# Seven block products for three of eight quads of the gate and up projections, five smaller feed-forward parts, and a scheduler that orders the feed-forward instructions

## The chip, the cores and the metric

The kernel runs on one core of a Trainium2 chip. The metric is the time of one execution on the device in microseconds (us); the median of several runs is given. A profile is one more execution, recorded by the hardware profiler. Engines are called PE (TensorE, matrix products), DVE (VectorE), ACT (ScalarE), POOL (GpSimd) and SP (SyncE, which issues the loads here).

## The reference

One layer of a transformer encoder on 256 tokens of 2048 features, all in float32. The first sub-layer mixes tokens (latent attention and dilated attention, gated and projected). The second, which the change is about, is a feed-forward block with 5632 hidden columns:

```python
gt, up = jnp.split(rms_norm(x, g_ffn) @ w_gate_up, 2, axis=-1)
return x + (jax.nn.silu(gt) * up) @ w_down
```

`w_gate_up` is 2048 x 11264 (the gate's 5632 columns, then the up columns), `w_down` is 5632 x 2048.

## The kernel before, in words

All float32 products are made of three matmuls. Each operand is cut in a high part of type float32r and a low part, which is what the cast left out. `mm3` (L383) multiplies high by high, high by low and low by high into one PSUM bank; the low by low term is left out.

Every weight product is a `Group`: up to 512 columns of a weight matrix, the list of its blocks of 128 rows (k), the transposed activation it multiplies and an `evac` function for the finished sums. A group holds two PSUM banks, one for each half of 128 tokens (the tag `main`, two tiles in turn, so that one group's sums can be read while the next ones grow). Groups are cut into chunks of two k: 512 KB of weights. `load(i)` (L694) issues a chunk's transfer on SP's queue. `split(i)` (L705) casts it on ACT (L710, the high part) and subtracts on DVE (L711, the low part). `products(i)` (L718) issues its 12 matmuls of 128x512 on PE: two k, two token halves, three matmuls. Loads run four chunks ahead of the products and splits three. There are four raw buffers, four for high parts and four for low ones; SP waits with a load until DVE has subtracted from the buffer's old content.

The feed-forward block comes last. The normalised activation is not scaled before the product; the row factor `st["2"]` is applied when the sums are read. `evac_wo` (L568) adds the residual to form `x1`, and a job transposes `x1` into `hT`, four feature blocks at a time (L201, eight transposes into a bank pair with the tag `side`). The 5632 hidden columns are worked through in 11 strips of 512, in two parts of six and five strips (`halves`). Each strip is a gate group of 16 k and an up group of 16 k. `evac_gate` (L592) applies Silu to the gate's sums on ACT, `evac_up` (L600) multiplies by the up sums on DVE, and a job transposes the result (the tile `tr_hid`, eight transposes) and cuts it into high and low parts (L171, L176). After a part's strips come four groups of `w_down`, 512 output columns each, whose k are the hidden blocks of that part; `evac_down` adds their sums to `x1`.

The order of all instructions is written out by hand: `tc.manual_schedule()` keeps every engine's instructions in the order of the program text, and the loop at the end of `layer_kernel` goes through the chunks, advancing at most one pending job after each.

Of the kernel before, what the change touches and what calls it, by code (L numbers as in the profile page):

```python
# [19 lines left out]
P = 128  # L20
# [17 lines left out]
CK = 2  # L38
AHEAD = 3
# [29 lines left out]

class Flag:  # L70
# [11 lines left out]
def layer_kernel(ctx: ExitStack, tc: tile.TileContext, a: dict, out: bass.AP):  # L82
    nc = tc.nc
    cp = ctx.enter_context(tc.tile_pool(name="cp", bufs=1))
    wp = ctx.enter_context(tc.tile_pool(name="wp", bufs=AHEAD + 1))
    tp = ctx.enter_context(tc.tile_pool(name="tp", bufs=34))
# [3 lines left out]
    ctx.enter_context(tc.manual_schedule())  # L90
# [4 lines left out]
    def small(shape, name):  # L95
        return cp.tile(shape, F32, name=name)

# [81 lines left out]

    class Act:  # L180
        """hi and lo parts of a transposed activation, in tiles of 4 blocks."""
# [14 lines left out]
    def transpose_in(act, k0, nk, src, gname=None):  # L196
        """blocks k0..k0+nk (nk <= 4, in one tile of act) from src(t, k) [tok, 128]."""
# [142 lines left out]
    def rope(x, A, B, nh, i):  # L340
        """x [P, NT, nh, 64] rotated in place, with the gain in the tables."""
# [46 lines left out]
    def job_attn(kind, p):  # L388
# [29 lines left out]
        # transposes of q and k  # L418
# [21 lines left out]
        # scores  # L440
# [28 lines left out]
        # transposes of the probabilities  # L469
# [8 lines left out]
        # values  # L478
# [8 lines left out]
    def job_prep_dil(n):  # L487
        """the norms of all heads: keys are scaled, the queries' factor waits for the scores"""
# [72 lines left out]
    x1, hT, hjobs, xres = {}, Act("hT", KD), {}, {}  # L561
    ss2 = small([P, NT, 4], "ss2")

    def load_xres(j):
        xres[j] = t4([P, NT, 512], f"xres{j}")
        nc.sync.dma_start(xres[j], xd[:, :, j * 512:(j + 1) * 512])

    def evac_wo(j):  # L568
        def evac(ps, step):
# [6 lines left out]
            def job():  # L576
                transpose_in(hT, 4 * j, 4, lambda t, k: x1[j][:, t, (k % 4) * P:(k % 4 + 1) * P], "g_ffn")
                return
                yield
            hjobs[j] = Job(job())  # L580
            hjobs[j].ready = step + 2
            jobs.append(hjobs[j])
# [7 lines left out]
    sg, hidT, djobs = {}, {}, {}  # L590

    def evac_gate(half, i):  # L592
        def evac(ps, step):
            z = t4([P, NT, 512], f"sg{half}_{i}")
            for t in range(NT):
                nc.scalar.activation(z[:, t], ps[:, t], AF.Silu, scale=st["2"][:, t:t + 1])
            sg[half, i] = z
        return evac

    def evac_up(half, i):  # L600
        def evac(ps, step):
            z = sg[half, i]
            for t in range(NT):
                nc.vector.scalar_tensor_tensor(z[:, t], ps[:, t], st["2"][:, t:t + 1], z[:, t], op0=ALU.mult, op1=ALU.mult)

            def job():
                transpose_in(hidT[half], 4 * i, 4, lambda t, k: z[:, t, (k % 4) * P:(k % 4 + 1) * P])
                return
                yield
            djobs[half, i] = Job(job())  # L610
            djobs[half, i].ready = step + 2
            jobs.append(djobs[half, i])
        return evac

    def evac_down(half, j):
        def evac(ps, step):
            nc.vector.tensor_add(x1[j], ps, x1[j])
            if half == 1:
# [20 lines left out]
    g_in(0, 512, evac_lat("cq"), sizes=[1, 1, 2, 2, 2, 2, 2, 2, 2])  # L639
# [28 lines left out]
    halves = (range(0, 6), range(6, 11))  # L668
    for half, js in enumerate(halves):
        hidT[half] = Act(f"hid{half}", 4 * len(js))  # L670
        for i, j in enumerate(js):
            nh = {k: (lambda k=k: [hjobs[k // 4]]) for k in range(KD)}
            groups.append(Group(W["w_gate_up"], 512 * j, 512, range(KD), hT, evac_gate(half, i), nh))
            groups.append(Group(W["w_gate_up"], DFF + 512 * j, 512, range(KD), hT, evac_up(half, i), nh))
# [5 lines left out]
    chunks = []  # L680
    for gi, g in enumerate(groups):
        ks, sizes = list(g.ks), list(g.sizes or [])
        while ks:
            n = sizes.pop(0) if sizes else CK
            chunks.append((g, gi, ks[:n], ks[0] == g.ks[0], len(ks) <= n))
            ks = ks[n:]

    wt, parts, gps = {}, {}, {}
    first_chunk = {}
    for i, c in enumerate(chunks):  # L690
        first_chunk.setdefault(c[1], i)
    early = {}

    def load(i):  # L694
        g, gi, ks, _, _ = chunks[i]
        if gi == 0 and i:
# [3 lines left out]
        t = wp.tile([P, len(ks), g.n], F32, name=f"w{i}", tag="w")  # L700
        src = g.w[ks[0] * P:(ks[-1] + 1) * P, g.c0:g.c0 + g.n]
        nc.sync.dma_start(t, src.rearrange("(k p) n -> p k n", p=P))
        wt[i] = t

    def split(i):  # L705
        g, gi, ks, _, _ = chunks[i]
        t = wt.pop(i)
        h = wp.tile([P, len(ks), g.n], F32R, name=f"wh{i}", tag="wh")
        l = wp.tile([P, len(ks), g.n], F32R, name=f"wl{i}", tag="wl")
# [146 lines left out]
```

## Time and profile before

| | |
|---|---|
| median of three runs | 1368.96 us (1368.63 to 1369.15) |
| profiled execution, span from the first to the last instruction | 1367.5 us |
| PE busy | 1356.5 us (99%) |
| DVE busy | 758.1 us (55%) |
| ACT busy | 623.5 us (46%) |
| read from HBM | 253.97 MB (187 GB/s over the span, writes included) |
| granted TensorE clock | 1.000 |

The profiled execution's own time is known by its span alone; the span leaves out what lies before the first and after the last instruction. Busy times are sums of an engine's instruction durations. A matmul's end is modelled and matmuls overlap, so PE's pace is read from the distance of their starts.

### The profile page before, as it was taken

How to read it: one execution, taken by the hardware profiler on the slowest of the kernel's cores; microseconds unless marked ns; L12 is line 12 of the kernel's file. 1: busy time of each engine (PE TensorE's matmuls, PEld its weight loads, DVE VectorE, ACT ScalarE, POOL GpSimd, SP SyncE). 2: the span in 40 equal slices, each digit the busy share in tenths (PEclk: the TensorE clock that was granted, in tenths of full speed). 3: DMA queues.
4: the chain of work that ended last, by engine and by line, in shares of the span. 5: the costliest groups of instructions: out<-in, count | busy, mean ns of one | idle time of the engine just before them, and what ended most of it. 6: DMA issues, size and time to landing. Idle time of an engine off the chain costs nothing.

```text
span 1367.5 us, 16361 instructions
## 1 busy us (share of the span) xinstructions
PE 1356.5 (99%) x6342; PEld 1144.7 (84%) x6342; DVE 758.1 (55%) x774; ACT 623.5 (46%) x776; POOL 32.3 (2%) x41
## 2 busy tenths in 40 slices
PE   7999999999999999999999999999999999999998
PEld 6899999888888888888888888888888888888887
DVE  5566777677655556555445544554444544555443
ACT  6555655454444444445444444433344444444332
POOL 1011111000000000000000000000000000000000
PEclk9999999999999999999999999999999999999999
DMA  8555555555566666565665665555665665565663
GB/s 259 175 173 168 158 172 177 174 166 172 178 202 199 198 190 216 193 210 181 196 192 182 191 198 184 187 189 193 194 193 187 194 197 188 186 188 183 202 212 123
DMA packets 138205, 257.14 MB, mean 188 GB/s; under 512 B 9192, under 2 KB 28688, under 8 KB 138128
## 3 DMA queue, kind: packets, MB, share of 16 engines
q1 hardware_dynamic: 137760, 255.96, 59.8%
q8 instruction: 49, 0.80, 0.2%
q14 instruction: 28, 0.23, 0.0%
q10 hardware_dynamic: 144, 0.13, 0.0%
q0 software_dynamic: 224, 0.01, 0.0%
HBM read 253.97 MB, written 2.10 MB: 187 GB/s over the span
## 4 chain that ended last, share of the span: by engine, by line
PE 99%; DMA 1%; SPq 0%; DVE 0%; issue 0%; ACT 0%; DVEq 0%
PE g L384 31%; PE g L386 31%; PE g L385 31%; PE tr_hid L201 1%; DMA w<-in_w_in_dram 1%; PE tr_hT L201 0%; PE tr_mT L201 0%; PE tr_xT L201 0%; DMA xn<-in_x_dram 0%; PE mla3s L386 0%; PE mla2s L386 0%; PE mla0s L386 0%; PE mla1s L386 0%; PE mla2s L385 0%; PE mla2s L384 0%; PE mla1s L385 0%
## 5 line engine op out<-in xcount | busy, mean ns | idle before, releaser
L711 DVE TENSOR_TENSOR wl<-w,wh 128x1024 fp32r<-128x1024 f32 (+2 forms) x481 | 575.6, 1201 | 472.8 <-ACT wh L710 470.8
L710 ACT CAST wh<-w 128x1024 fp32r<-128x1024 f32 (+2 forms) x481 | 496.2, 1036 | 537.6 <-PE g L386 489.7
L384 PE MATMUL g<-wh,hTh 128*128 128x512 f32 x704 | 274.8, 390 | 0.0
L386 PE MATMUL g<-wh,hTl 128*128 128x512 f32 x704 | 274.0, 389 | 0.0
L385 PE MATMUL g<-wl,hTh 128*128 128x512 f32 x704 | 273.9, 389 | 0.0
L384 PE MATMUL g<-wh,xTh 128*128 128x512 f32 (+1 forms) x544 | 210.2, 386 | 1.9 <-ACT xTh L173 1.9
L386 PE MATMUL g<-wh,xTl 128*128 128x512 f32 (+1 forms) x544 | 207.2, 381 | 0.5 <-DVE xTl L178 0.5
L385 PE MATMUL g<-wl,xTh 128*128 128x512 f32 (+1 forms) x544 | 207.2, 381 | 0.0
L386 PEld LDWEIGHTS g<-wh,hTl 128*128 128x128 f32 x704 | 132.1, 188 | 27.6
L385 PEld LDWEIGHTS g<-wl,hTh 128*128 128x128 f32 x704 | 132.2, 188 | 27.1
L384 PEld LDWEIGHTS g<-wh,hTh 128*128 128x128 f32 x704 | 132.2, 188 | 27.1
L384 PEld LDWEIGHTS g<-wh,xTh 128*128 128x128 f32 x544 | 102.7, 189 | 17.2 <-ACT xTh L173 2.1
L386 PEld LDWEIGHTS g<-wh,xTl 128*128 128x128 f32 x544 | 102.4, 188 | 17.3 <-DVE xTl L178 1.0
L385 PEld LDWEIGHTS g<-wl,xTh 128*128 128x128 f32 x544 | 102.6, 189 | 15.3 <-DVE wl L711 0.4
L384 PE MATMUL g<-wh,hid0h 128*128 128x512 f32 x192 | 74.8, 390 | 0.0
L386 PE MATMUL g<-wh,hid0l 128*128 128x512 f32 x192 | 74.7, 389 | 0.0
L385 PE MATMUL g<-wl,hid0h 128*128 128x512 f32 x192 | 74.7, 389 | 0.0
L384 PE MATMUL g<-wh,hid1h 128*128 128x512 f32 x160 | 62.3, 390 | 0.0
L386 PE MATMUL g<-wh,hid1l 128*128 128x512 f32 x160 | 62.2, 389 | 0.0
L385 PE MATMUL g<-wl,hid1h 128*128 128x512 f32 x160 | 62.2, 389 | 0.0
L384 PE MATMUL g<-wh,mTh 128*128 128x512 f32 x128 | 50.2, 392 | 0.0
L386 PE MATMUL g<-wh,mTl 128*128 128x512 f32 x128 | 49.8, 389 | 0.0
(509 smaller groups left out, 1233.5 us busy)
## 6 DMA issues: line engine op xcount, KB each, us to landing
w<-in_w_gate_up_dram SPq DMA_DIRECT2D x176, 512.0 KB, 4.5
w<-in_w_down_dram SPq DMA_DIRECT2D x88, 512.0 KB, 4.3
w<-in_w_in_dram SPq DMA_DIRECT2D x79, 512.0 KB, 4.2
w<-in_w_in_dram SPq DMA_DIRECT2D x56, 448.0 KB, 3.6
w<-in_w_o_dram SPq DMA_DIRECT2D x32, 512.0 KB, 4.5
w<-in_w_o_mla_dram SPq DMA_DIRECT2D x16, 512.0 KB, 4.1
w<-in_w_o_dil_dram SPq DMA_DIRECT2D x16, 512.0 KB, 4.2
w<-in_w_ukv_dram SPq DMA_DIRECT2D x8, 512.0 KB, 4.3
```

The source lines that it names most:

```text
L201: nc.tensor.transpose(ps[:, k, t * P:(t + 1) * P], src(t, k0 + k), ident)
L384: nc.tensor.matmul(ps, ah, bh, start=first, stop=False)
L385: nc.tensor.matmul(ps, ah, bl, start=False, stop=False)
L386: nc.tensor.matmul(ps, al, bh, start=False, stop=last)
L710: nc.scalar.copy(h, t)
L711: nc.vector.tensor_sub(l, t, f32(h))
```

## The change

The feed-forward block is rearranged; the arithmetic of everything before it stays.

- Gate and up of a strip become one group, a *pair*. Its work is cut into eight *quads*: two feature blocks by two token halves on the activation's side, two feature blocks by gate and up on the weights' side. That is a product of two 2 x 2 block matrices. Five quads are done plainly with eight block products. Three (`FAST`, quads 2, 4 and 6) are done with seven block products of sums and differences of blocks (Winograd's form of Strassen's method), each still three matmuls. The last quad, 7, is a plain one.
- The sums and differences of the activation's blocks are made once, in `job_h`. Those of the weights are made for each fast quad in `split_fast`: four adds of 512 elements on DVE, in place in the raw buffer, after the two right-hand blocks and one left-hand block were cut into high and low parts.
- A pair holds all eight PSUM banks (`hold_banks`): four for the ordinary sums, into which three of the seven products go too, and four shared by the other products of the three fast quads. `evac_fast` combines the shared four, placed after the last fast quad; `evac_pair` adds the result to the ordinary four, then applies Silu and multiplies.
- Five parts of 3, 2, 2, 2 and 2 strips take the place of two of 6 and 5. Down groups use the held banks, two groups chunk by chunk in turn (not the very last two).
- A feed-forward chunk is 1 MB (a quad, or four k of `w_down`) in two transfers. There are three raw buffers of 1 MB, and six of the same size for high and low parts. Before the feed-forward block a chunk stays 512 KB; there it uses half of a raw buffer, and one of the six buffers holds its high and low part. The working tiles `t4` go from 34 to 28.
- From the third of the four `w_o` groups on the hand-written order ends (`in_order.close()`): the framework's scheduler orders the instructions of each engine by their place in the text, their readiness and a priority, which is raised by `PRIO` for the combining.

```diff
-CK = 2
-AHEAD = 3
+CK = 4
+AHEAD = 2
+PARTS = ((0, 3), (3, 5), (5, 7), (7, 9), (9, 11))
+PRIO = 200
+NPAIR = KD // 2
+FAST = (2, 4, 6)
...
+class Quad:
+    def __init__(self, group, i):
+        self.group, self.i, self.fast = group, i, i in FAST
+        plain = [k for k in range(NPAIR) if k not in FAST]
+        self.first, self.last = i == plain[0], i == plain[-1]
+        self.first_fast, self.last_fast = i == FAST[0], i == FAST[-1]
...
-    wp = ctx.enter_context(tc.tile_pool(name="wp", bufs=AHEAD + 1))
-    tp = ctx.enter_context(tc.tile_pool(name="tp", bufs=34))
+    tp = ctx.enter_context(tc.tile_pool(name="tp", bufs=28))
+    xp = ctx.enter_context(tc.tile_pool(name="xp", bufs=3))
+    wp = ctx.enter_context(tc.tile_pool(name="wp", bufs=6))
     sp = ctx.enter_context(tc.tile_pool(name="sp", bufs=4))
     psm = ctx.enter_context(tc.tile_pool(name="psm", bufs=2, space=PSUM))
     pss = ctx.enter_context(tc.tile_pool(name="pss", bufs=2, space=PSUM))
-    ctx.enter_context(tc.manual_schedule())
+    in_order = ctx.enter_context(ExitStack())
+    in_order.enter_context(tc.manual_schedule())
...
+    def half_side(name):
+        if not held:
+            return side(name)[:, :512]
+        spare.rotate(-1)
+        return held["q"][spare[-1]]
+    def hold_banks():
+        for n in "AB":
+            held[n] = psm.tile([P, NT, 512], F32, name=f"m{n}", tag="main")
+        for n in "CD":
+            held[n] = side(f"s{n}").rearrange("p (t n) -> p t n", t=NT)
+        held["q"] = {m: held[n][:, i] for n, ms in (("A", (1, 6)), ("B", (7, 5)), ("C", (3, 2)), ("D", (4, 0)))
+                     for i, m in enumerate(ms)}
+        spare.extend((1, 6, 7, 5))
...
+    def split_pair(h, l, x):
+        nc.scalar.copy(h, x)
+        nc.vector.tensor_sub(l, x, f32(h))
...
+    def job_h(i):
+        ps = half_side(f"tr_h{i}").rearrange("p (k s) -> p k s", s=S)
+        for k in range(2):
+            f = 2 * i + k
+            for t in range(NT):
+                nc.tensor.transpose(ps[:, k, t * P:(t + 1) * P], x1[f // 4][:, t, (f % 4) * P:(f % 4 + 1) * P], ident)
+        g = [gain("g_ffn", 2 * i + k) for k in range(2)]
+        if i not in FAST:
+            hP[i] = t4([P, 2, 2, S], f"hP{i}", F32R)
+            split_evac(*((hP[i][:, 0, k], hP[i][:, 1, k], ps[:, k], g[k]) for k in range(2)))
+        else:
+            v, l, h = t4([P, 8, P], f"hs{i}"), t4([P, 7, P], f"hsl{i}", F32R), t4([P, 7, P], f"hsh{i}", F32R)
+            nc.scalar.activation(v[:, 0:8:7], ps[:, 0].rearrange("p (t s) -> p t s", t=NT), AF.Copy, scale=g[0])
+            nc.scalar.activation(v[:, 1:3], ps[:, 1].rearrange("p (t s) -> p t s", t=NT), AF.Copy, scale=g[1])
+            nc.vector.tensor_sub(v[:, 3], v[:, 7], v[:, 2])
+            nc.vector.tensor_sub(v[:, 4], v[:, 7], v[:, 0])
+            nc.vector.tensor_sub(v[:, 5], v[:, 0], v[:, 3])
+            nc.vector.tensor_sub(v[:, 6], v[:, 1], v[:, 5])
+            split_pair(h, l, v[:, :7])
+            hq[i] = (h, l)
...
+    def evac_fast(q):
+        bank, z, u = held["q"], t4([P, NT, 512], f"z{q.group.c0}"), t4([P, NT, 512], f"u{q.group.c0}")
+        add, sub = nc.vector.tensor_add, nc.vector.tensor_sub
+        with tc.high_priority(offset=PRIO):
+            nc.scalar.copy(u[:, 0], bank[1])
+            sub(z[:, 0], bank[6], u[:, 0])
+            add(u[:, 1], bank[7], z[:, 0])
+            add(z[:, 1], bank[5], u[:, 1])
+            add(z[:, 0], bank[5], z[:, 0])
+        q.group.zu = z, u
+    def evac_pair(half, i, last):
+        def evac(zu, step):
+            q = held["q"]
+            z, u = zu
+            add, sub = nc.vector.tensor_add, nc.vector.tensor_sub
+            with tc.high_priority(offset=PRIO):
+                add(z[:, 1], q[0], z[:, 1])
+                add(z[:, 0], q[3], z[:, 0])
+                add(u[:, 0], q[2], u[:, 0])
+                sub(u[:, 1], q[4], u[:, 1])
+            r = st["2"]
+            for t in range(NT):
+                nc.scalar.activation(z[:, t], z[:, t], AF.Silu, scale=r[:, t:t + 1])
+            for t in range(NT):
+                nc.vector.scalar_tensor_tensor(z[:, t], u[:, t], r[:, t:t + 1], z[:, t], op0=ALU.mult, op1=ALU.mult)
 
             def job():
-                transpose_in(hidT[half], 4 * i, 4, lambda t, k: z[:, t, (k % 4) * P:(k % 4 + 1) * P])
+                ps = held["D" if last else "A"].rearrange("p t (k s) -> p (t k) s", s=S)
+                for k in range(4):
+                    for t in range(NT):
+                        nc.tensor.transpose(ps[:, k, t * P:(t + 1) * P], z[:, t, k * P:(k + 1) * P], ident)
+                h, l = hidT[half].tiles(i)
...
+            needs = {k: (lambda k=k: [hjobs[k]]) for k in range(NPAIR)}
+            needs[FAST[0]] = lambda: list(hjobs.values())
+            if i:
+                needs[FAST[0]] = lambda half=half, i=i: [djobs[half, i - 1]]
+            groups.append(Group(W["w_gate_up"], 512 * j, 1024, range(NPAIR), None, evac_pair(half, i, i == len(js) - 1), needs))
...
+        elif gi >= ffn_at:
+            for two in (gi, gi + 2):
+                for a_, b_ in zip(chunk_ks(groups[two], two), chunk_ks(groups[two + 1], two)):
+                    if two + 2 == len(groups):
+                        continue
+                    add_chunk(two, a_)
+                    add_chunk(two + 1, b_)
+            if two + 2 == len(groups):
+                for e in (two, two + 1):
+                    for ks in chunk_ks(groups[e], e):
+                        add_chunk(e, ks)
+            gi += 3
...
+    def load(c):
+        g, gi, ks, q = chunks[c]
+        t = xt[c] = xp.tile([P, 4, 512], F32, name=f"x{c}", tag="x")
+        if q:
+            for kk in range(2):
+                src = g.w[(2 * q.i + kk) * P:(2 * q.i + kk + 1) * P].rearrange("p (n f) -> p n f", n=2)
+                nc.sync.dma_start(t[:, 2 * kk:2 * kk + 2], src[:, :, g.c0:g.c0 + 512])
+            return
...
+    def split_fast(c):
+        x = xt[c]
+        rh, rl, r = (t4([P, 2, 512], f"{n}{c}", F32R) for n in ("rh", "rl", "r"))
+        split_pair(rh, rl, x[:, 2:4])
+        split_pair(r[:, 0], r[:, 1], x[:, 1])
+        add = nc.vector.tensor_add
+        add(x[:, 1], x[:, 0], x[:, 1])
+        add(x[:, 0], x[:, 0], x[:, 2])
+        add(x[:, 2], x[:, 1], x[:, 2])
+        add(x[:, 3], x[:, 2], x[:, 3])
+        raws[c] = {1: (r[:, 0], r[:, 1]), 3: (rh[:, 0], rl[:, 0]), 2: (rh[:, 1], rl[:, 1])}
+    def split(c):
+        g, gi, ks, q = chunks[c]
+        if q and q.fast and c not in raws:
+            split_fast(c)
+        t = xt.pop(c)
+        h = w8(f"wh{c}")
+        h, l = (h, w8(f"wl{c}")) if gi >= ffn_at else (h[:, :2], h[:, 2:])
+        s = (slice(None), slice(0, 4 if q else len(ks)), slice(0, 512 if q else g.n))
+        split_pair(h[s], l[s], t[s])
+        if q and q.fast:
+            parts[c] = raws.pop(c) | {m: (h[:, n], l[:, n]) for n, m in enumerate((7, 5, 6, 4))}
+        else:
+            parts[c] = (h, l)
...
+    FACTOR = {1: 0, 2: 1, 4: 2, 5: 3, 7: 4, 6: 5, 3: 6}
+    PLAIN = {(0, 0): 3, (0, 1): 2, (1, 0): 0, (1, 1): 4}
+    def products_quad(c):
+        q = chunks[c][3]
+        bank, w = held["q"], parts.pop(c)
+        if not q.fast:
+            h, l = w
+            for t, n in ((1, 0), (0, 0), (0, 1), (1, 1)):
+                m = PLAIN[t, n]
+                for kk in range(2):
+                    s = slice(t * P, (t + 1) * P)
+                    mm3(bank[m], hP[q.i][:, 0, kk, s], hP[q.i][:, 1, kk, s], h[:, 2 * kk + n], l[:, 2 * kk + n],
+                        q.first and kk == 0, q.last and kk == 1)
+        else:
+            h, l = hq[q.i]
+            for m in (1, 6, 7, 5, 3, 2, 4):
+                f = FACTOR[m]
+                mm3(bank[m], h[:, f], l[:, f], *w[m], q.first_fast and m in (1, 5, 6, 7), q.last_fast and m in (1, 5, 6, 7))
+        if q.last_fast:
+            evac_fast(q)
+        return getattr(q.group, "zu", None)
+    DOWN = "ABCA"
...
+            ps = held[DOWN[g.c0 // 512]]
...
+    def splits(to):
+        while ahead["split"] < min(to, n):
+            c = ahead["split"]
+            loads(c + 1)
+            if c + 1 < n and chunks[c + 1][3] and chunks[c + 1][3].fast and c + 1 not in raws:
+                loads(c + 2)
+                split_fast(c + 1)
+            split(c)
+            ahead["split"] += 1
...
+        if first and gi == ffn_at - 2:
+            in_order.close()
         for fn in early.get(i, ()):
             fn()
-        if i + AHEAD + 1 < n:
-            load(i + AHEAD + 1)
-        if i + 1 < n and chunks[i][1] == 0:
+        if ks[0] == allks[0]:
+            loads(c + AHEAD + 2)
+        if i + 1 < len(steps) and gi == 0:
             for j in needs_of(i + 1):
                 j.finish(i)
         for j in needs_of(i):
             j.finish(i)
-        if i + AHEAD < n:
-            split(i + AHEAD)
+        if ks[0] == allks[0]:
+            ahead_of = c + AHEAD + 1 + (gi < ffn_at - 1)
+            splits(ahead_of)
+            loads(ahead_of + 2)
+        if gi == ffn_at and not held:
+            hold_banks()
```

## Rows read from the trace of the kernel before

**Rows 1.** The page's busy times: us, share of the span, instructions.
```profile
PE 1356.5 (99%) x6342; PEld 1144.7 (84%) x6342; DVE 758.1 (55%) x774; ACT 623.5 (46%) x776; POOL 32.3 (2%) x41
```
**Rows 2.** The page's chain that ended last, share of the span by engine.
```profile
PE 99%; DMA 1%; SPq 0%; DVE 0%; issue 0%; ACT 0%; DVEq 0%
```
**Rows 3.** Stretches: us, busy (instructions) PE, PEld, DVE, ACT, POOL; clock; DMA; GB/s.
```profile
60.00:1363.00 1303.00, 1303.00 (x6105) 1102.37 (x6104) 724.32 (x725) 588.82 (x714) 26.07 (x23) 1.00 0.60 187
...
907.00:950.00 43.00, 43.00 (x193) 35.65 (x192) 21.26 (x18) 17.79 (x17) 0.00 (x0) 1.00 0.59 189
```
**Rows 4.** The chain in order of time, two sets of transposes: start, us, what.
```profile
862.14 0.87 PE tr_hid L201 x8
...
906.55 0.87 PE tr_hid L201 x8
```
**Rows 5.** The page's groups, feed-forward matmuls: out<-in, count, busy us, mean ns.
```profile
L384 PE MATMUL g<-wh,hTh 128*128 128x512 f32 x704 | 274.8, 390 | 0.0
L386 PE MATMUL g<-wh,hTl 128*128 128x512 f32 x704 | 274.0, 389 | 0.0
L385 PE MATMUL g<-wl,hTh 128*128 128x512 f32 x704 | 273.9, 389 | 0.0
...
L384 PE MATMUL g<-wh,hid0h 128*128 128x512 f32 x192 | 74.8, 390 | 0.0
...
L384 PE MATMUL g<-wh,hid1h 128*128 128x512 f32 x160 | 62.3, 390 | 0.0
```
**Rows 6.** Waits: who waited for whom, us in total, times, longest us.
```profile
ACT wh L710 <- PE g L386: 489.7, 322, 4.4
DVE wl L711 <- ACT wh L710: 470.8, 330, 7.0
```
**Rows 7.** Groups by form, DVE: count, busy us, mean ns, idle before.
```profile
L711 DVE TENSOR_TENSOR wl<-w,wh 128x1024 fp32r<-128x1024 f32 x415 | 506.6, 1224 | 457.0 <-ACT wh L710 455.7
...
L604 DVE SCALAR_TENSOR_TENSOR sg<-g,r,sg 128x512 f32<-128x512 f32 x22 | 15.5, 747 | 4.6 <-PE g L386 4.6
...
L617 DVE TENSOR_TENSOR x<-g,x 128x1024 f32<-128x1024 f32 x7 | 8.6, 1224 | 2.9 <-PE g L386 2.9
...
L711 DVE TENSOR_TENSOR wl<-w,wh 128x512 fp32r<-128x512 f32 x2 | 1.4, 692 | 1.3 <-ACT wh L710 1.3
```
**Rows 8.** Groups by form, ACT: the same columns.
```profile
L710 ACT CAST wh<-w 128x1024 fp32r<-128x1024 f32 x415 | 436.1, 1054 | 511.7 <-PE g L386 465.3 <-DMA w<-in_w_down_dram 28.9 <-DMA w<-in_w_in_dram 10.9
...
L596 ACT ACTIVATE sg<-g,r 128x512 f32<-128x512 f32 x22 | 13.9, 686 | 16.7 <-PE g L386 16.7
...
L173 ACT ACTIVATE hTh<-tr_hT,gcol 128x256 fp32r<-128x256 f32 x16 | 6.3, 475 | 7.3 <-PE tr_hT L201 7.3
L171 ACT CAST hid0h<-tr_hid 128x1024 fp32r<-128x1024 f32 x6 | 6.1, 1018 | 15.3 <-PE tr_hid L201 15.3
...
L710 ACT CAST wh<-w 128x512 fp32r<-128x512 f32 x2 | 1.2, 616 | 1.2 <-DMA w<-in_w_in_dram 1.2
```
**Rows 9.** Timeline, DVE around 901 and 1362 us: start, us, instruction.
```profile
901.15 1.41 DVE L604 SCALAR_TENSOR_TENSOR sg<-g,r,sg 128x512 f32<-128x512 f32 x2 [0.41 <-PE g L386]
...
1362.14 0.69 DVE L626 TENSOR_TENSOR x<-g,x 128x512 f32<-128x512 f32 x1 [6.47 <-PE g L386]
```
**Rows 10.** Waits of SP's queue, the longest: us in total, times, longest us.
```profile
SPq L702 <- DVE wl L711: 1008.2, 442, 5.6
```
**Rows 11.** Transfers: KB each, median us to landing; then GB/s in 0:40 us.
```profile
w<-in_w_gate_up_dram SPq DMA_DIRECT2D x176, 512.0 KB, 4.5
...
GB/s 0 8 157 298 185 142 262 313 323 388 394 388 383 375 376 368 379 370 374 375 378 385 227 168 346 98 281 156 53 238 344 67 50 144 258 195 287 195 272 197
```
**Rows 12.** Timeline of SP's queue, the fourth and fifth weight load: start, us.
```profile
4.63 0.47 SPq L702 DMA_DIRECT2D w<-in_w_in_dram  x1
...
6.11 0.86 SPq L702 DMA_DIRECT2D w<-in_w_in_dram  x1
```

More of the change, by code (lines that the diff above doesn't have):

```diff
@@ L678, in layer_kernel, with add_chunk @@
                                 {k: (lambda k=k, half=half: [djobs[half, k // 4]]) for k in range(4 * len(js))}))
-    chunks = []
-    for gi, g in enumerate(groups):
-        ks, sizes = list(g.ks), list(g.sizes or [])
+    chunks, steps = [], []
+    def add_chunk(gi, ks, q=None):
+        g = groups[gi]
+        c = len(chunks)
+        chunks.append((g, gi, ks, q))
+        if q:
+            steps.append((c, ks, ks[0] == g.ks[0], ks[-1] == g.ks[-1]))
+            return
+        for o in range(0, len(ks), 2):
+            sub = ks[o:o + 2]
+            steps.append((c, sub, sub[0] == g.ks[0], sub[-1] == g.ks[-1]))
@@ L694, in load @@
-    def load(i):
-        g, gi, ks, _, _ = chunks[i]
-        if gi == 0 and i:
+        return r
+    gi = 0
+    while gi < len(groups):
+        g = groups[gi]
+        if g.n == 1024:
+            for i in g.ks:
+                add_chunk(gi, [i], Quad(g, i))
+        elif gi >= ffn_at:
[11 more added lines that the diff above has]
+        else:
+            for ks in chunk_ks(g, gi):
+                add_chunk(gi, ks)
+        gi += 1
@@ L699, in load @@
                 load_rows()
[L700 to L709, printed above, removed]
-        nc.scalar.copy(h, t)
-        nc.vector.tensor_sub(l, t, f32(h))
-        parts[i] = (h, l)
+        for o in range(0, len(ks), 2):
+            sub = ks[o:o + 2]
+            src = g.w[sub[0] * P:(sub[-1] + 1) * P, g.c0:g.c0 + g.n]
+            nc.sync.dma_start(t[:, o:o + len(sub), :g.n], src.rearrange("(k p) n -> p k n", p=P))
@@ L718, in products @@
+    DOWN = "ABCA"
     def products(i):
-        g, gi, ks, first, last = chunks[i]
+        c, ks, first, last = steps[i]
+        g, gi, allks, q = chunks[c]
+        if q:
+            return products_quad(c)
         final = gi == len(groups) - 1
-        if first and not final:
+        if first and gi < ffn_at:
             ps = psm.tile([P, NT, 512], F32, name=f"g{gi}", tag="main")
@@ L770, in layer_kernel, with loads @@
     n = len(chunks)
-    for i in range(min(AHEAD + 1, n)):
-        load(i)
+    ahead = {"load": 0, "split": 0}
+    def loads(to):
+        while ahead["load"] < min(to, n):
+            load(ahead["load"])
+            ahead["load"] += 1
+    def splits(to):
[7 more added lines that the diff above has]
+            ahead["split"] += 1
+    loads(3)
     xjobs[0].finish(0)
-    for i in range(min(AHEAD, n)):
-        split(i)
-        if i + 1 < 2:
-            xjobs[i + 1].finish(0)
+    splits(1)
+    xjobs[1].finish(0)
+    splits(2)
     jobs.extend((gains, xstat))
@@ L780, in layer_kernel @@
     xstat.ready = 2
-    for i in range(n):
+    for i, (c, ks, first, last) in enumerate(steps):
+        g, gi, allks, q = chunks[c]
+        if first and gi == ffn_at - 2:
+            in_order.close()
         for fn in early.get(i, ()):
             fn()
-        if i + AHEAD + 1 < n:
-            load(i + AHEAD + 1)
-        if i + 1 < n and chunks[i][1] == 0:
+        if ks[0] == allks[0]:
+            loads(c + AHEAD + 2)
+        if i + 1 < len(steps) and gi == 0:
             for j in needs_of(i + 1):
@@ L790, in layer_kernel @@
             j.finish(i)
-        if i + AHEAD < n:
-            split(i + AHEAD)
+        if ks[0] == allks[0]:
[4 more added lines that the diff above has]
+            hold_banks()
         ps = products(i)
-        g, gi, _, _, last = chunks[i]
         if last and gi < len(groups) - 1:
```

85 lines of the change are left out of this document (43 added, 42 removed).

## The prediction

> **What bounds the kernel now.** I read the page's engine list first: PE is busy 1356.5 of 1367.5 us, DVE 55%, ACT 46% [rows 1]. The chain that ended last is PE for 99% [rows 2]. A busy PE need not be a PE at its pace, so next I took the stretches: from 60 us to 1363 us PE has no gap at all, at granted clock 1.00, the higher level, 2.4 GHz [rows 3]. Its pace stands in the chain in order of time: from one set of eight hidden transposes to the next are 44.41 us [rows 4], and the code puts 192 matmuls and those eight transposes (0.87 us) there, so one 128x512 matmul costs (44.41 - 0.87) / 192 = 0.2268 us from start to start. The 0.39 us in the groups [rows 5] is one matmul's modelled length; they overlap, and 0.39 must not be used as a price. The waits show the other engines waiting for PE: ACT's weight casts 489.7 us, and DVE's subtractions 470.8 us behind those casts [rows 6]. So only fewer matmuls help, and only while DVE, ACT, the loads and the PSUM banks keep up with a PE that asks sooner.
>
> **Matmuls removed.** An FFN pair (512 gate columns and the 512 up columns beside them) is now 16 blocks of features x 2 token halves x 2 sides x 3 matmuls = 192, and 11 pairs are the 2112 of [rows 5]. A quad is two feature blocks by gate and up by two token halves: plain 8 products = 24 matmuls, fast 7 = 21. Three fast quads save 9 per pair: 11 x 9 x 0.2268 = 22.5 us. Transposes stay: 32 of h, 88 of the hidden blocks. The down product keeps its 1056 matmuls. The pair becomes 183 x 0.2268 + 0.87 = 42.4 us of PE, a plain quad 5.44, a fast one 4.76.
>
> The Trainium skill ("TensorE: Matmul & The Clock Gate", "Back-to-back issue gap") gives about 131 ns as the sustained spacing at 512 columns; by it the saving would be 13.0 us, by its isolated formula (215.8 ns) 21.4. The trace's 226.8 ns differs from both, and the row decides.
>
> **Work added on DVE and ACT.** DVE takes 1.224 us for 1024 elements and 0.692 for 512 [rows 7], so 1.04 ns per further element; 2048 in one instruction: 2.29 us (estimate). ACT's cast takes 1.054 and 0.616 [rows 8]; 2048: 1.93. A plain quad costs DVE 2.29 us. A fast one: the right-hand pair's low part 1.22, the raw block's 0.69, four adds of 512 at 0.69, the four sums' low part 2.29, together 6.97. Per pair five plain and three fast quads: 32.4 us. Then eight PSUM combinations of 512: the nearest rows are one 512-wide add from PSUM at L626, 0.69 [rows 9], and one with a factor, 0.747 [rows 7]; I take 0.69, 5.5 us. With two gate multiplications (1.5) and the hidden low part (1.2) DVE has 40.6 us per pair, against 21.3 in 43 us now [rows 3]. Neighbouring DVE instructions overlap by 0.08 us (two of 0.747 take 1.41, [rows 9]); over 37 instructions that is 3 us, so 37.5 to 40.6 against PE's 42.4: **DVE comes to 88 to 96% of PE while a pair runs**. ACT has 5 x 1.93 + 3 x 3.60 + 0.6 + 1.4 + 1.0 = 23.5 us; it stays free.
>
> What hides this is PE itself. In the down stretches DVE has slack: per pair 4 splits of 2048 (9.2 us) plus the additions to x1 (4 x 1.22 per part) against 96 x 0.2268 = 21.8 us. And the six split buffers hold two quads ahead of the one in use, 10.9 us of PE work, refilled in each of the five down stretches. A part of two pairs is late only when DVE's time per pair, waits included, passes 42.4 + 10.9 / 2 = 47.8 us (three pairs: 46.0). I cost the added DVE work at 0; with that cover gone it costs 1 us per us.
>
> **PSUM.** A pair now holds all eight banks: four for the ordinary sums, four that the seven-product quads share. The combining of the four shared ones starts when the last fast quad has nine matmuls to go, and runs beside the last quad (ACT copy 0.6, four DVE adds 2.8). The four final adds then free the ordinary banks in the order in which that last quad finishes them and the next pair's first quad wants them: each bank is done 18 matmuls (4.1 us) before it is wanted, less 0.69 for the add: 3.4 us of slack, so one split of 2.29 in front on DVE is covered, two are not. Bounds 0 to 2.8 us per pair (all four adds exposed); I take 0.2, nearest to 0 as the adds carry priority: 11 x 0.2 = 2.2 us.
>
> **First pair.** Its first fast quad waits for all eight transposed h jobs; the last two come after two quads, into banks that the fast quad wants: two casts of 256 (2 x 0.475, [rows 8]) and a little DVE. Bounds 0 to 3; I take 1.5.
>
> **Part ends.** Of a two-pair part the last hidden block is wanted after two down chunks, 10.9 us. It needs add 0.7, two Silu 1.4, two multiplications 1.5, transposes 0.9, cast 1.0, low part 1.2 = 6.7, and up to two splits in front (4.6): 11.3. Bounds 0 to 3 per part; I take 0.4 x 5 = 2.
>
> **Loads.** The bytes stay. Three raw buffers of 1 MB take the place of four of 512 KB; SP issues a load when DVE's subtraction frees the buffer [rows 10], and a 512 KB load lands 4.5 us after issue [rows 11]. A pair's 8 MB in 42.4 us are 198 GB/s, against up to 394 in the first 40 us [rows 11]. At the start the fourth weight load goes out at 4.63 us and the fifth only when the first buffer is free, 6.11 [rows 12]; now the fourth must wait for that, 1.5 us later, while the transfers are the bound anyway. Bounds -1 to 2; I take 0. Ahead of the FFN split buffers go from four to six and work tiles from 34 to 28: PE waits nowhere there now, bounds 0 to 3, I take 0.
>
> **Sum.** Span 1367.5 - 22.5 + 2.2 + 1.5 + 2 = 1350.7. The page gives the profiled execution only by its span; the median of the runs is 1.5 us above it, which I add for what lies around: **1352 us**.
>
> **Rivals.**
> *DVE is starved by its own loads (slower).* Place: fast and plain quads in turn, three times per pair. In written order the next fast quad's raw split comes before the plain quad's, and with three raw buffers its load starts only when the previous plain quad's subtraction ends. Then load 4.5 + cast 1.05 - the 2.29 of the subtraction that lies between = 3.3 us of idle DVE, 9.8 per pair: 50.4 against 42.4. Less the 10.9 of lead per part: 11 x 8.0 - 5 x 10.9 = 34 us, so 1380; with 1 MB landing 1.4 us later (at 385 GB/s) 1427. It decides from 47.8 us per pair. For: the sum is 96% before any wait. Against: the plain quad's data has landed by then, and the scheduler may put its subtraction first.
> *Banks.* Two splits or a whole fast block sit in front of the final adds: 1.4 to 3.8 us per pair, 1362 to 1388. For: there is no second set of banks, which the kernel has now (two main tiles in turn). Against: 3.4 us of slack and the priority. The Trainium skill has the rule ("Perfetto Trace Analysis", "Matmuls"): independent groups should rotate through different banks, so that one's evacuation lies beside the next one's matmuls. A pair in all eight breaks it between pairs. With all four adds exposed, 11 x 2.8 = 31 us, the time is 1346.5 + 31 = 1377, slower; the trace now agrees with the rule in that PE has no gap.
> *Part ends and first pair* at their upper bounds: 5 x 3 + 3 = 18, 1365: most of the gain lost, still no loss.
>
> **How the numbers follow.** Forecast 0.60 (own range 1346 to 1361), part ends 0.10, banks 0.13, starved DVE 0.17. A measurement tells 0.2% (2.7 us) from no change. Faster: 0.60 + 0.10 and 0.02 from the mild ends of the others, 0.72; no change 0.07; slower 0.21 (most of the starved case, half of banks). Below 1346 and above 1385 I leave 0.16, mostly the starved case.
>
> **What would show it.** PE with 99 fewer matmuls of 512 columns and a spacing near 0.227 us; DVE near 90% in a pair and half of that in a down stretch; raw splits waiting for ACT, not for loads. Wrong if PE waits for the sums' low part in every fast quad (starved), or for the adds from PSUM at each pair's first quad (banks), or if the granted clock leaves 1.00 after such gaps.

## The result, and the profile after

The changed kernel takes 1359.26 us (median of four, 1356.11 to 1361.27) against 1369.06 before: ratio 0.9923 [0.9909, 0.9937]. Run again on another chip it took 1357.24 against 1370.43: 0.9908 [0.9895, 0.9922]. It is 10 to 13 us faster; the forecast was 1352. The profiled execution's span is 1354.3 us, its time 1356.11.

The page after: busy times and the chain that ended last, by engine. They answer to [rows 1, 2].

```profile
PE 1339.5 (99%) x6243; PEld 1126.0 (83%) x6243; DVE 949.1 (70%) x949; ACT 652.2 (48%) x724; POOL 34.3 (3%) x41
...
PE 94%; DVE 2%; issue 1%; DMA 1%; ACT 1%; SPq 0%; DVEq 0%; ACTq 0%
```

99 matmuls are gone (6342 to 6243), DVE has 191 us more, and PE's share of the chain fell from 99% to 94%. The span fell by 13.2 us where 99 x 0.2268 are 22.5. So 9.2 us were given back in this execution, and about 3 more in the median. Two stretches, one pair and one two-pair part; columns as in [rows 3]:

```profile
722.00:765.00 43.00, 43.00 (x194) 35.49 (x193) 38.59 (x38) 21.78 (x18) 0.00 (x0) 1.00 0.59 196
...
830.50:914.90 84.40, 84.24 (x375) 69.41 (x374) 70.85 (x66) 41.06 (x31) 0.00 (x0) 1.00 0.59 199
```

In the first stretch DVE is busy for 38.6 of 43 us, 90%, where it was 21.3 [rows 3]: the forecast said 88 to 96%. Over the whole two-pair part it is 70.85 of 84.40, 84%, and in the down stretch behind it (914.92 to 960.55) 29.5 of 45.63 us, 65% where the forecast said half: part of the pairs' work on DVE is done there. From transposes to transposes, the chain in order of time, a pair with its wait at the start takes 42.95 us (42.4 forecast, 44.41 in [rows 4]):

```profile
689.94 0.87 PE mA L691 x8
...
732.89 0.87 PE mA L691 x8
```

The durations that had no row before (groups by form; count, busy us, mean ns, idle before): the subtraction of 2048, one of the weight adds, an add of 512 from PSUM, and the cast on ACT.

```profile
L221 DVE TENSOR_TENSOR wl<-x,wh 128x2048 fp32r<-128x2048 f32 x132 | 300.8, 2289 | 134.5 <-ACT wh L220 132.7 <-PE g L429 1.0
...
L845 DVE TENSOR_TENSOR x<-x 128x512 f32<-128x512 f32 x33 | 22.8, 691 | 0.9
...
L665 DVE TENSOR_TENSOR u<-mB,z 128x512 f32<-128x512 f32 x11 | 7.6, 692 | 1.2
...
L220 ACT CAST wh<-x 128x2048 fp32r<-128x2048 f32 x131 | 248.3, 1910 | 310.4 <-DVE x L847 127.7 <-PE mA L428 58.1 <-PE mB L428 29.7
```

All are as estimated, to 1% (2.29, 0.69, 0.69, 1.93). What PE waited for in the feed-forward part (us in total, times, longest); there was no such wait before:

```profile
PE sD L691 <- DVE z L685: 1.7, 2, 1.0
PE sC L427 <- DVE u L679: 1.5, 5, 0.9
PE mA L619 <- ACT hs L627: 0.9, 1, 0.9
PE mA L427 <- DVE x L712: 0.8, 1, 0.8
```

In this order: a part's last transposes wait for the second gate multiplication; a pair's first quad for the final adds; the last h transposes for the casts of the h job before; the tail's second half for the reading of the first. A wait is counted only beyond the modelled end of the matmul ahead (0.39 us after its start), so measure by starts. From the first matmul of each stretch to that of the next (from the trace's start times, us; two-pair parts: mean of four; down stretches of 192 matmuls: mean of the first three; the last one runs to the span's end). Two-pair parts and down stretches are those behind the first part and its own, longer down stretch (66.2 us at pace). "At pace" is 0.2268 per matmul and 0.87 per eight transposes.

```
                         first part  two-pair part  down   last down
three fast, at pace         127.1        83.9       44.4
the change                  129.7        84.6       45.3     49.7
again (e1)                  132.0        84.7       44.8     50.0
no fast quads (e2)          135.8        88.5       44.4     49.7
  at pace                   133.2        88.0
two fast (e3)               134.2        87.0       44.4     49.7
  at pace                   129.2        85.2
doubled subtraction (e5)    140.4        93.8       44.5     50.6
hand order (e6)             168.8       101.4       44.4     49.7
ordinary banks (e4)         132.2        84.5       45.3     50.6
halves (e7)                 131.8        85.4       44.4     49.7
three waits mended (e8)     132.1        85.0       44.4     48.6
part ends and tail (e10)    132.0        84.7       44.4     48.6
banks, halves too (e11)     128.4        84.9       44.4     48.6
the same, four fast (e12)   127.0        83.4       44.4     48.8
  at pace                   125.1        82.5
```

The 9 us of the change: 2.6 in the first part, 4 x 0.7 in the others, 3 x 0.9 in down stretches, 1.1 at the tail. The waits at the six pair ends that another pair follows are 2.6 us of it by starts: 0.3 us five times and 1.05 once. DVE's timeline around 868 us shows one of the five:

```profile
868.09 0.68 DVE L667 TENSOR_TENSOR z<-mB,z 128x512 f32<-128x512 f32 x1
868.69 2.28 DVE L221 TENSOR_TENSOR wl<-x,wh 128x2048 fp32r<-128x2048 f32 x1
870.89 0.68 DVE L678 TENSOR_TENSOR z<-sC,z 128x512 f32<-128x512 f32 x1
871.49 0.68 DVE L679 TENSOR_TENSOR u<-sC,u 128x512 f32<-128x512 f32 x1
```

PE's last matmul of this pair in tile sC starts at 870.41; as modelled it ends at 870.80. DVE has just finished a 2.28 us split (870.97), and the first add starts 0.09 us after that end. Where DVE had been free (e7, at 765.41) an add starts 0.04 us after it, so the split costs next to nothing here. Both adds of sC end at 872.17. PE wanted sC again at 872.0, six matmuls after it had left it: the scheduler's order left 1.4 us of slack where the text's order has 18 matmuls, 4.1 us. The two adds alone take 1.28 of the 1.4, and the end of the matmul and the hand-overs come on top: that makes the 0.3 us. In e2, with DVE busy for 40.9 of 88.4 us, five of the six waits are as long (0.37). Only in the longest wait does a split hold the adds:

```profile
999.45 2.29 DVE L221 TENSOR_TENSOR wl<-x,wh 128x2048 fp32r<-128x2048 f32 x1 [0.65 <-ACT wh L220]
1001.65 0.69 DVE L678 TENSOR_TENSOR z<-sC,z 128x512 f32<-128x512 f32 x1
...
1003.08 0.47 PE L427 MATMUL sC<-wh,hP 128*128 128x512 f32 x1 [0.89 <-DVE u L679]
```

There the last matmul in sC ended at 1000.83, and the first add starts 0.82 us later.

### The profile page after: what moved, and what is told of

Read it like the earlier page. It is cut to its first block, busy times and chain, and to the rows that moved or that the text cites. A ratio compares the mean times of both kernels' runs of the same rounds, so it can differ in the third digit from the quotient of the medians.

```text
span 1354.3 us, 16169 instructions
## 1 busy us (share of the span) xinstructions
PE 1339.5 (99%) x6243; PEld 1126.0 (83%) x6243; DVE 949.1 (70%) x949; ACT 652.2 (48%) x724; POOL 34.3 (3%) x41
## 4 chain that ended last, share of the span: by engine, by line
PE 94%; DVE 2%; issue 1%; DMA 1%; ACT 1%; SPq 0%; DVEq 0%; ACTq 0%
PE g L429 14%; PE g L427 14%; PE g L428 13%; PE sC L427 6%; PE sC L429 6%; PE sC L428 6%; PE mA L427 4%; PE mA L429 4%; PE mA L428 4%; PE sD L429 4%; PE sD L427 4%; PE sD L428 4%; PE mB L428 3%; PE mB L429 3%; PE mB L427 3%
## 5 line engine op out<-in xcount | busy, mean ns | idle before, releaser
L220 ACT CAST wh<-x 128x1024 fp32r<-128x1024 f32 (+3 forms) x349 | 465.3, 1352 | 437.0 <-DVE x L847 127.7
L221 DVE TENSOR_TENSOR wl<-x,wh 128x2048 fp32r<-128x2048 f32 x132 | 300.8, 2289 | 134.5 <-ACT wh L220 132.7
L221 DVE TENSOR_TENSOR wh<-x,wh 128x1024 fp32r<-128x1024 f32 (+2 forms) x217 | 250.6, 1172 | 113.1 <-ACT wh L220 111.9
L427 PE MATMUL g<-wh,xTh 128*128 128x512 f32 (+1 forms) x544 | 210.6, 387 | 0.6 <-ACT xTh L212 0.6
L428 PE MATMUL g<-wh,xTh 128*128 128x512 f32 (+1 forms) x544 | 207.9, 382 | 0.0
L427 PEld LDWEIGHTS g<-wh,xTh 128*128 128x128 f32 x544 | 102.8, 189 | 15.9 <-ACT xTh L212 0.9
L428 PEld LDWEIGHTS g<-wh,xTh 128*128 128x128 f32 x544 | 102.9, 189 | 15.4 <-DVE wh L221 0.4
L427 PE MATMUL sC<-wh,hP 128*128 128x512 f32 x220 | 86.1, 391 | 1.6 <-DVE u L679 1.5
L429 PE MATMUL sC<-wh,hP 128*128 128x512 f32 x220 | 85.7, 390 | 0.0
L429 PE MATMUL sD<-wh,hP 128*128 128x512 f32 x220 | 85.7, 389 | 0.0
L428 PE MATMUL sC<-wl,hP 128*128 128x512 f32 x220 | 85.7, 389 | 0.0
L427 PE MATMUL sD<-wh,hP 128*128 128x512 f32 x220 | 85.7, 389 | 0.0
L428 PE MATMUL sD<-wl,hP 128*128 128x512 f32 x220 | 85.7, 389 | 0.0
L220 ACT CAST rh<-x 128x1024 fp32r<-128x1024 f32 x33 | 34.7, 1051 | 36.1 <-DMA x<-in_w_gate_up_dram 36.1
L427 PEld LDWEIGHTS sC<-wh,hP 128*128 128x128 f32 x220 | 41.3, 188 | 12.3 <-issue 4.0
L427 PE MATMUL g<-wh,mTh 128*128 128x512 f32 x128 | 50.5, 394 | 0.0
L428 PE MATMUL g<-wh,mTh 128*128 128x512 f32 x128 | 49.9, 390 | 0.0
L427 PEld LDWEIGHTS sD<-wh,hP 128*128 128x128 f32 x220 | 41.3, 188 | 8.6
```

What stands on the lines that cost most here:

```text
L220: nc.scalar.copy(h, x)
L221: nc.vector.tensor_sub(l, x, f32(h))
L427: nc.tensor.matmul(ps, ah, bh, start=first, stop=False)
L428: nc.tensor.matmul(ps, ah, bl, start=False, stop=False)
L429: nc.tensor.matmul(ps, al, bh, start=False, stop=last)
```

## The experiments

Each ratio is against the kernel before, run on the same chip.

**e1, the change again.** 

> The changed kernel once more, unedited. Theory A (99 matmuls saved, 22.5 us; about 9 us given back in short PE gaps at pair ends, part ends, the first pair and the tail; the rest of the distance to the forecast is a granted clock under 1.00 in some executions): times between 1356 and 1361.5, and where the profiled execution has a mean clock of 0.997 to 0.999, a stretch at the lower clock of 3 to 8 us in all, behind a PE gap in the feed-forward part. Theory B (the spread comes from DVE or the loads being late by another amount each time): the clock is 1.00 throughout and the PE gaps differ in length by 3 to 5 us between this profile and the first.

1357.24 us, 0.9908. Stretches of it, columns as in [rows 3], the clock third from the end:

```profile
640.00:653.00 13.00, 11.09 (x53) 8.95 (x53) 10.62 (x10) 7.38 (x11) 2.12 (x2) 1.00 0.50 166
653.40:656.70 3.30, 3.30 (x10) 2.53 (x9) 2.21 (x7) 2.03 (x4) 0.00 (x0) 0.50 0.46 128
657.00:670.00 13.00, 13.00 (x59) 10.76 (x58) 10.01 (x11) 6.44 (x5) 0.00 (x0) 1.00 0.34 121
```

PE idled 1.9 us of the first 13, and its clock was at the lower level (1.2 GHz) for 3.4 us behind that. There its matmuls start 0.43 us apart:

```profile
652.11 0.66 PE L619 MATMUL mA<-ident,x 128*128 128x128 f32 x4 [1.91 <-ACT hs L627]
...
654.09 0.63 PE L428 MATMUL sD<-wl,hP 128*128 128x512 f32 x1
654.51 0.63 PE L429 MATMUL sD<-wh,hP 128*128 128x512 f32 x1
```

That costs (0.427 - 0.227) x 8 = 1.6 us. A second such stretch lies at 15 us, where PE starts and waits. So theory A holds as far as this profile goes: a longer gap in front of the h transposes (2.1 us by starts, 1.0 in the first profile) and two low stretches are most of what makes this span 3.2 us longer than the first; the part ends took 1.6 us less. The clock alone does not order the executions: two of this run at mean clocks of 0.999 and 1.000 took 1356.17 and 1358.07 us.

**e2, no fast quads.** `FAST = ()`, Silu and the multiplication read the four banks. 

> No fast quads: all eight quads of a pair plain (192 matmuls again), Silu and the multiplication read the four banks directly; five parts, held banks, 1 MB chunks and the scheduler stay. If the 9 to 12 us that were given back belong to the new structure (order, held banks, parts): 1359.3 + 22.5 = 1382 us or a few less. If they belong to DVE's extra work for the fast quads: 1369 to 1371 us. Theory A, in which both the order and DVE's queue take part: between, 1373 to 1378, with the waits at the part ends still there.

1374.97 us, 1.0036 [1.0023, 1.0048]: the new structure alone costs 4.5 us, in six waits at pair ends (2.6 us counted, 3.6 by starts) and the tail (0.95). The down stretches run at pace, so the expected waits at the part ends are not there without fast quads. From there the three fast quads bring 1374.97 - 1357.24 = 17.7 of 22.5 us. Between the two pure theories, nearer the second, as theory A had it.

**e3, two fast quads.** `FAST = (2, 4)`. 

> Two fast quads of eight (2 and 4) in place of three: 33 matmuls come back, 7.5 us of PE; DVE loses 4.7 us per pair. If PE sets the time and what was given back does not hang on DVE's load: 1359.3 + 7.5 = 1367. If DVE's load makes the loss: it falls by a third or more, 1360 to 1363. If DVE is the bound outright: no slower than the change, 1356 to 1360.

1369.74 us, 0.9998 [0.9989, 1.0007]: slower than all three expectations. With less work (62.9 of 86.3 us in a two-pair part) DVE keeps PE waiting longer, 1.2 to 1.5 us at every pair end in the parts after the first. Its queue around 876 us:

```profile
876.07 2.28 DVE L221 TENSOR_TENSOR wl<-x,wh 128x2048 fp32r<-128x2048 f32 x1
878.27 0.69 DVE L845 TENSOR_TENSOR x<-x 128x512 f32<-128x512 f32 x1
878.88 0.68 DVE L678 TENSOR_TENSOR z<-sC,z 128x512 f32<-128x512 f32 x1
879.48 0.68 DVE L679 TENSOR_TENSOR u<-sC,u 128x512 f32<-128x512 f32 x1
```

A split and a weight add stand in front of the adds that PE needs. With 33 matmuls more to do PE loses more time to waiting, so what is given back does not go by DVE's sum but by the order in its queue.

**e4, banks.**

```diff
-        held["q"] = {m: held[n][:, i] for n, ms in (("A", (1, 6)), ("B", (7, 5)), ("C", (3, 2)), ("D", (4, 0)))
+        held["q"] = {m: held[n][:, i] for n, ms in (("A", (1, 6)), ("B", (7, 5)), ("C", (2, 4)), ("D", (0, 3)))
```

> The four ordinary banks share their two tiles otherwise: 0 with 3 and 2 with 4, in the order in which a plain quad fills them; nothing else. Theory A: the framework treats the two banks of a tile as one dependency, so that the adds of the tile with 0 and 4 wait for the whole last quad; with 0 and 3 together one tile is done 12 matmuls (2.7 us) before the next pair wants it, and the waits at the pair ends (2.6 us in the profile, 0.3 to 1.05 each) go: 2 to 4 us faster than the change, some 1356. Rival (DVE has a 2.3 us split in front of the adds, whatever the tile): the waits stay, time as the change, 1359.

1358.78 us, 0.9920 [0.9906, 0.9933]: no gain. The waits at the pair ends stay at 0.3 us by starts (0.5 and 1.2 once each), though a tile is now left 12 matmuls before it is wanted. Here a split does stand in front: at 873.83 PE waits for adds that begin at 872.40, behind a split from 870.20 on, where the tile was done at 870.95. That is the rival's picture.

**e5, subtraction doubled.**

```diff
         if q and q.fast:
+            nc.vector.tensor_sub(l[s], t[s], f32(h[s]))
             parts[c] = raws.pop(c) | {m: (h[:, n], l[:, n]) for n, m in enumerate((7, 5, 6, 4))}
```

> Every fast quad's 2.29 us low part of the sums is subtracted a second time into the same place: 6.9 us more DVE work per pair, 45.5 us against PE's 42.4 (75 us over 11 pairs). Lead theory (DVE is covered by two quads of lead, refilled in each down stretch, and a two-pair part is late only from 47.8 us per pair): up to 2 us per part, 0 to 10 us slower than the unedited change, 1358 to 1368. Rival (DVE already sets the pace in a pair): the excess over PE is paid in full, 3 us x 11 and more, 1390 and up; with DVE as the outright bound 1358 + 75 = 1433.

1401.42 us, 1.0231 [1.0217, 1.0245]: 42 us are paid of the 73 by which DVE's busy time in the feed-forward part grew (540.5 to 613.3). The lead theory falls in this form. A two-pair part and the longest wait of PE:

```profile
841.65:934.14 92.49, 86.63 (x376) 70.43 (x374) 82.81 (x72) 41.03 (x31) 0.00 (x0) 0.98 0.51 172
```
```profile
PE sC L427 <- DVE u L679: 23.6, 6, 4.2
```

DVE's 82.8 us are just under PE's 83.9 at pace (99%), and the part takes 92.5: it is not the sum that is paid, but the final adds, which come after the splits in the queue. The clock was low for 23.9 us in all behind such waits; at e1's rate (1.6 us lost in 3.4) that costs some 11 us (estimate).

**e6, hand order to the end.** `in_order.close()` taken out. 

> The hand-written order stays to the end: the scheduler orders nothing, the priorities do nothing. The prediction's starved-DVE rival (in text order the next fast quad's raw split stands in front of the plain quad's, and waits for its load) gives 1380 to 1427 us, with DVE waiting 3 to 5 us for the raw cast in front of each fast quad. If the scheduler's order brings nothing: 1356 to 1360. My own expectation is 1380, PE waiting for the sums' low part.

1460.88 us, 1.0661 [1.0646, 1.0676]. The direction was right, the size far off: the final adds are late at every pair end (up to 6.0 us) and the low clock covers 82 us. ACT's raw casts wait for their loads 31 times, 81.3 us in all (36.1 us in the change), as the rival says, but the largest wait of PE is that for the adds:

```profile
PE sD L427 <- DVE u L680: 35.8, 6, 6.0
```

So the scheduler is worth some 100 us here; without it the change would be 90 us slower than before.

**e7, halves.** Every 2048-element cast and subtraction in two of 1024. 

> Each 2048-element cast and subtraction of the feed-forward part is done in two halves of 1024 (1.05 and 1.22 us). DVE gets 0.16 us more per split, some 1.3 us per pair. Theory (the waits at the pair ends come from one undivided 2.29 us subtraction that DVE has begun when the last quad's banks become ready): these waits shrink from 0.3 to 1.3 us to under 0.3 each, 2 to 3 us faster than the unedited change, 1355. Rival (DVE's sum counts): 0 to 14 us slower.

1361.59 us, 0.9944 [0.9930, 0.9957]: 2 us slower, if anything; the theory's 1355 was missed. The new order has longer waits at the pair ends (0.7 to 2.4 us by starts), while the down stretches run at pace; with six matmuls of slack smaller pieces alone don't help.

**e8, three waits, and e10, two of them.** The first edit is in e8 alone.

```diff
-        spare.extend((1, 6, 7, 5))
+        spare.extend((1, 7, 6, 5))
...
-            djobs[half, i].ready = step + 2
+            djobs[half, i].ready = step + (3 if last else 2)
...
-            gps[gi] = [ps, ps[:, 0], ps[:, 1]]
+            gps[gi] = [ps, ps[:, 0], held["D"][:, 0] if final else ps[:, 1]]
```

> Three waits taken by their causes: the last two h jobs transpose into banks of different tiles; a part's last hidden block is transposed one step (six or so matmuls) later; the last group's second token half gets a bank of another tile. If the framework treats the two banks of a tile as one dependency, the 1 to 2 us gap in front of the last h transposes goes, and with it the stretch at half clock behind it (1.6 us where it occurs), and the 0.95 us at the tail; the later transposes take 1 to 2 us of waits. Sum: 3 to 6 us faster than the unedited change, 1352 to 1355. Rival (these waits only hide one behind another, DVE being late anyway): 1358 to 1360, the gaps moved to the next matmul.

> Only two of the three edits of the kernel with three waits taken: the part's last hidden block one step later, and the tail's second half in another tile; the h transposes stay. In that kernel every down stretch ran at PE's pace (44.41 us) and the tail had no gap, 3.7 us in all, but the first part took 2.4 us more. If the h edit made that loss: 1358 - 3.7 = 1354. If the scheduler's new order at the pair ends makes it (1.6 us in two pairs): 1356 to 1358.

e8: 1356.98 us, 0.9901 [0.9887, 0.9915], between its two ranges; e10: 1354.90, 0.9891 [0.9878, 0.9905]. PE's waits in the feed-forward part of e10:

```profile
PE mA L619 <- ACT hs L627: 1.9, 1, 1.9
PE sC L427 <- ACT z L683: 1.3, 1, 1.3
PE sC L427 <- DVE u L679: 0.6, 4, 0.2
```

In both kernels the waits of the transposes and of the tail are gone; down stretches take 44.4 us, PE's pace, and the last one 48.6. The tail shows that two banks of one tile were one dependency: with the second half in another tile its wait is gone. The h edit only moved its wait behind the transposes (2.1 us at `mA L427`): in the first part DVE and ACT are late as such. In the profile of the unedited change the chain leaves PE after 617 us for a load of 5.96 us, casts and subtractions, and comes back at 649.5. e10's time is that of the expectation's first branch, but its reason is not shown: the first part takes 132.0 us without the h edit, a low stretch among them, and 132.1 with it.

**e9, the weight adds on POOL.** `add = nc.gpsimd.tensor_add` in `split_fast`. 

> The four adds of a fast quad's weight blocks run on the idle POOL in place of DVE: 8.3 us less DVE work per pair (38.6 to about 30 us against PE's 42.4). Theory after the doubled subtraction (whatever DVE is late with is paid at the pair ends, where the final adds queue behind it): the waits at the pair ends (2.3 to 2.6 us in sum) and in front of the first products shrink to under 1 us in sum, and the low clock behind them goes: 2 to 5 us faster than the unedited change, some 1354. Rival (the order in DVE's queue alone makes the waits, not its load): unchanged, 1357 to 1359. A third way: POOL takes 1 us and more for 512 elements or slows DVE beside it, the sums come late, and PE waits for the sums' low part: over 1365.

1459.27 us, 1.0655 [1.0641, 1.0670], the third way, and far over it:

```profile
L844 POOL TENSOR_TENSOR x<-x 128x512 f32<-128x512 f32 x32 | 70.7, 2210 | 520.3 <-DVE r L221 323.4 <-DMA x<-in_w_gate_up_dram 196.9
L847 POOL TENSOR_TENSOR x<-x 128x512 f32<-128x512 f32 x32 | 52.8, 1650 | 2.5
L846 POOL TENSOR_TENSOR x<-x 128x512 f32<-128x512 f32 x32 | 48.8, 1524 | 2.5
L845 POOL TENSOR_TENSOR x<-x 128x512 f32<-128x512 f32 x32 | 45.0, 1405 | 2.5
```

Four adds take 6.8 us in a row (2.8 on DVE), and the sums come late: PE waits 63 us for their casts. It says nothing on DVE's load.

**e11, banks and halves on top of e10.** 

> The two edits of the part ends and the tail, with the ordinary banks 0 and 3 in one tile and 2 and 4 in the other, and casts and subtractions in halves. A tile of two banks is then done 12 matmuls (2.7 us) before the next pair wants it, and no more than 1.22 us of subtraction can stand in front of its two adds (1.4 us): 2.6 us, so the waits at the pair ends should be 0 to 0.1 us each. 1352 to 1354. Rival (the waits are DVE's load, which the halves raise by 1.3 us per pair): waits of 0.5 to 1.5 us, 1357 or more.

1353.94 us, 0.9886 [0.9873, 0.9900], as forecast, but 1 us below e10 is inside the intervals: neither edit helped alone, and that they help together is not shown by the time. The first part fell from 132.0 to 128.4 us (the gap at the h transposes and the low clock behind it did not come in this profile), the two-pair parts did not (84.7 and 84.9). Four of the six pair ends have no wait now; the other two wait 0.8 and 1.2 us by starts.

**e12, four fast quads in e11.** `FAST = (2, 3, 5, 6)`. 

> The best kernel so far (banks 0 with 3 and 2 with 4, halves, the later hidden transposes, the tail's other tile) with four fast quads of eight, 2, 3, 5 and 6: 33 matmuls of 512 fewer, 7.5 us of PE, and 4.7 us more DVE work per pair, some 43 us against PE's 41.7 (40 in 42.4 with three). If PE's pace sets the time: 1354 - 7.5 = 1346.5. If DVE's work is paid once it comes near PE's, as with the doubled subtraction (6.9 us per pair added, 42 us lost): 4.7 / 6.9 of that, 29 us, less 7.5: 1375. I expect 1365 to 1380, with PE waiting for low parts of sums and at the pair ends, and stretches at the lower clock.

**1344.53 us, 0.9820 [0.9807, 0.9834]**: 24.7 of the 30 us that 132 fewer matmuls are worth, the best of all, and against my expectation. A stretch in a two-pair part, and PE's waits:

```profile
830.00:912.00 82.00, 81.86 (x365) 67.29 (x364) 78.01 (x92) 43.86 (x49) 0.00 (x0) 1.00 0.61 204
```
```profile
PE mA L428 <- DVE wl L221: 1.1, 3, 0.4
PE sD L427 <- DVE z L678: 0.7, 2, 0.5
```

DVE is busy for 95% and PE keeps its pace to 1%. So a DVE at 95% costs next to nothing by itself. The scaling from e5 was wrong. e5 had undivided splits and PE's order with six matmuls of slack, which is the likely cause; but its DVE work was also nearer to PE's (99% of its pace against 96% here), and no run tells the two apart.

## Why the prediction was right, and where its sizes were off

- **Matmuls removed: right.** 99 x 0.2268 us; the pair's 42.4 measured 42.95 with its wait.
- **Work on DVE: right in size in the densest stretch** (38.6 per pair against 37.5 to 40.6; [rows 7] carried to 2048 and 512 elements), 84% and not 88 to 96 over a two-pair part. **The cover was described wrongly.** "Late only from 47.8 us per pair" took the lead in split quads for cover of everything. e5, at 45.5 us by the same count, paid 42 us: the final adds cannot be done ahead, and a lead means splits in front of them. e12 shows that a load of 95% is covered.
- **Banks: the mechanism right, the slack wrong.** The prediction had 4.1 us less one add of 0.69, that is 3.4 us of slack, from the text's order. The scheduler put the tile filled last but one first in the next pair and left 1.4, and PE waits for both adds of the tile, 1.28. So there is no slack at all even with nothing in front. The term was 2.2 us for eleven pairs; six pair ends measured 2.6, and smaller delays in the two-pair parts 0.8. The rule quoted there from the Trainium skill ("Perfetto Trace Analysis", "Matmuls"), that independent groups should rotate through different banks, is borne out in mild form: e2, which gave up the second set of banks and the old order (and has the new parts and chunks), waits at each of the six pair ends, 3.6 us by starts, against none before.
- **First pair 1.5:** 2.6 measured in the first part of the first profile, 2.0 without its two pair ends; 4.9 in all in e1's with the low clock.
- **Part ends 2:** 2.7 in the down stretches. The term put the risk in the wanted hidden block; what came was transposes that PE's fixed order held before their input was ready.
- **Tail, no term:** 1.1. The last group's halves share a tile now, where they had two.
- **Start 0:** right, the first h transposes, in the second `w_o` group, start at 572.16 against 572.06 before, in the chain's view of [rows 4].
- **Sum.** The 5.7 us forecast as given back became 9.2, by small misses in nearly every term: 0.4 at the pair ends, 0.8 elsewhere in the two-pair parts, 0.5 in the first part, 0.7 at the part ends, 1.1 at the tail. About 3 us more lie between the profiled execution and the median, and the sum had no term for them; together they make the 7 us between 1352 and 1359. The four executions have spans of 1354.3 to 1359.5 us at mean clocks of 1.000 to 0.997. A mean clock of 0.999, as the two middle ones have, is worth 0.001 x 1357 = 1.4 us (estimate); the rest of the 3 is not explained.
- **Starved DVE (1380 to 1427):** not in the change, whose order is the scheduler's. In text order (e6) it is there and dearer, 1461, above all at the pair ends.
- **Luck has a share.** The sum has no term for the scheduler's order, and that order decides: e3, with 66 matmuls fewer than the kernel before (15.0 us) and less work on DVE, kept less than 1 us of them.

Open: how much of e12's ease comes from the halves, the banks or the part ends; they were not tried singly with four fast quads. Whether the spread of all executions is low clock alone: e1's profile shows low stretches for a part of it, and no run settles the rest.

## What to carry to other kernels

Where a change takes work from the bound engine and gives it to another, the second engine's total decides less than what stands in its queue in front of the result that frees a buffer. When all accumulators are held, read the bound engine's actual order in which it returns to them, not the text's, and set that slack against all reads of the buffer (here two adds of a tile, 1.28 us in 1.4) and what can stand in front of them. Piece size and buffer order did not help one at a time here. Before judging a load to be the limit, try one more unit of it in the mended order: four fast quads beat three.

## What was not expected of the hardware

A PE gap of 2.1 us (by starts) was followed by 3.4 us at the lower clock in e1 and e10 and by none in e8 and e7, with gaps of 2.3 and 2.4 us; why is open. Such a stretch costs 1.6 us, most of the gap again. POOL takes 1.4 to 2.2 us for an add of 512 float32 elements per partition, DVE 0.69.
